# DeltaNet layer on one core: the solve's closing operations inside the scan's last step, and three matmul inputs at another offset

## The chip, the core and the metric

The kernel runs on one core of a Trainium2 chip. A core has five engines that each run their own list of instructions in order: PE (TensorE, matmuls into PSUM; PEld is its weight load), DVE (VectorE), ACT (ScalarE), POOL (GpSimd) and SP (SyncE, which issues the DMAs here). An instruction waits for semaphores that other engines or DMAs raise, and all that stands behind it on its engine waits with it. The metric is the device time of one execution in microseconds (us).

## What is computed

One transformer layer with a DeltaNet branch: 512 latent tokens, 256 context tokens, width 1024, everything in float32. The part that the change touches, cut from the reference:

```python
kk = jnp.einsum('bhncd,bhnsd->bhncs', k, k)
a_mat = jnp.where(strict, beta[..., :, None] * dec * kk, 0.0) + jnp.eye(GDN_CHUNK, dtype=jnp.float32)
uw = lax.linalg.triangular_solve(a_mat, rhs, left_side=True, lower=True, unit_diagonal=True)   # per chunk
def step(s, inp):                                                   # the scan over chunks
    delta = u_c - jnp.einsum('bhcd,bhde->bhce', w_c, s)
    s_new = gl_c[..., None, None] * s + jnp.einsum('bhcd,bhce->bhde', kd_c, delta)
    o = jnp.einsum('bhcd,bhde->bhce', qd_c, s) + jnp.einsum('bhcs,bhse->bhce', p_c, delta)
    return s_new, o
y = (jax.nn.sigmoid(g_a) * (attn @ w_pa) + jax.nn.sigmoid(g_d) * (gdn @ w_pd)) @ w_out         # output projection
x = x + g2 * ((jax.nn.silu(g) * val) @ w_down)                      # second MLP stage, after u = conv(h @ w_up)
```

The scan runs in both directions for 8 heads.

## The kernel before

Every large product is three matmuls: an fp32 value is split into a rounded part and a rest (hi and lo, tiles `whi`, `wlo` for weights; two halves for the moving input), and `mm3` sums hi·hi, hi·lo and lo·hi. The 128-column weight tiles come one after another by DMA (`wraw`); ACT makes `whi`, DVE makes `wlo`.

The program first makes modulations and normed inputs, then attention. After it comes the DeltaNet part, for the heads in four pairs p = 0 to 3, with 128-token chunks (6 for a pair and direction). A pair goes through two stages:

- `gdn_solve` and `gdn_solved` invert the 32x32 diagonal blocks of the triangular matrices. `gdn_solve` builds `C`, `X` and `R` (each 128x1024) and then runs 31 rounds of a product (`prod`) and a sum into `R`; these rounds are on POOL for the pairs 1 to 3. `gdn_solved` closes it with three operations on DVE: `R` times `gT`, and two block transposes of `R` into the tiles `o_tr` and `o_nt`. Then `gdn_inv` puts the blocks together to full inverses (tile `TTm`) with many small matmuls. It begins with 192 matmuls of 32x32 that read `o_tr`, `o_nt` and `NN` and write four PSUM banks.
- `gdn_scan` goes through six steps. In a step DVE makes `r`, PE makes `TTm` times `r` (bank `pds`), DVE copies that to `dl`, and PE makes `qT` times the state (bank `pq`), which DVE scales and adds into `oacc` (the first output sum, L117). In steps 4 and 5 PE multiplies the masks `M` with `dl` (bank `pe`) and DVE adds that into `oacc` (the second output sum, L108).

The PSUM tiles of both stages come from one ring of four banks (`pbank`, tag `pb`). The banks that `gdn_inv` takes first are those that the last scan step's `pq` and `pe` held, so that the first round of the 32x32 matmuls needs `o_tr`, `o_nt` and both output sums.

The solve of pair p+1 runs beside the inversion of pair p, and its rounds go on under the scan of pair p. What stands here as a *handover* is the place where the scan of pair p ends and the inversion of pair p+1 begins; there are three (p = 0 to 1, 1 to 2, 2 to 3). Between these pieces `weave` puts matmuls of the other projections on PE (`mb`, moving inputs `hxH`, `hxL`, then `at`), a fixed number per piece; it leaves none between the last `pe` matmuls and the first 32x32 matmuls. `put` pins the closing operations at their place in program order; much else on DVE, ACT, POOL and SP is placed by a scheduler.

After the pairs come the two branch projections (moving inputs `at` for attention, `g_*` for DeltaNet), the output projection (moving input `y`, matmuls into `mc`), the MLP's first stage (moving input `h`) and its second (moving input `a`). `two(pool, k, by, name)` makes the hi and lo halves of such an input: 2 x k rows of 2048 bytes in a partition, in one tile aligned to 2048 bytes, which begin `by` bytes behind the tile's start. `h` has 192, `y` 64 and `a` 256; `at` for heads 4 to 7 is a plain tile, thus 0.

Of the kernel before, what the change touches and what calls it, by code (L numbers as in the profile page):

```python
# [6 lines left out]
F32 = mybir.dt.float32  # L7
# [7 lines left out]
P = 128  # L15
D = 1024
KT = 8
# [61 lines left out]
def hybrid_layer_body(tc, x, ctxt, xT, consts, cols, rows, w_mod1, w_mod2, w_db, w_aq, w_cm, w_pa, w_pd, w_out,  # L79
# [54 lines left out]
    with es:  # L134
# [805 lines left out]
                        tt(R[:, j + 1:32, 0:n], R[:, j + 1:32, 0:n], pv, ALU.add, eng)  # L940
            pre.append(R)

        def gdn_solved(pre, keep):
            kT, gT, NN, R = pre
            put = tc.keep_in_program_order if keep else lambda i: i
            with solver():
                put(V.tensor_tensor(out=R, in0=R, in1=gT.unsqueeze(2).to_broadcast([P, 32, 32]), op=ALU.mult))
                outs = [gq.tile([P, 32, 32], F32, name=nm, align_bytes=2048, tag="q4", bufs=3) for nm in ("o_tr", "o_nt")]
                for o, r in zip(outs, (R, R.rearrange("p i k -> p k i"))):
                    put(V.transpose(o.rearrange("p u s -> p s u"), r))  # L950
            pre[3:] = outs

        def gdn_inv(p, pre):
            kT, gT, NN, o_tr, o_nt = pre
# [66 lines left out]
        def gdn_scan(p, pre, seqs, nxt):  # L1021
# [29 lines left out]
            for st in range(6):  # L1051
                lat = st >= 2
                if st == 2:
                    oacc = gpool[0].tile([P, 2, 4, P], F32, name="oacc", tag="oacc")
                pks, pds, rs_ = [None, None], [None, None], [None, None]
                for d in range(2):
                    c = seq[d][st]
                    if S[d] is not None:
                        pks[d] = pbank()
                        for hh in range(2):  # L1060
                            mm(pks[d][:, hh, :], kT[:, hh, c * P:(c + 1) * P], S[d][:, hh, :])
                if st > 0:
                    yield WS[0]
                for d in range(2):
                    c = seq[d][st]
                    if S[d] is not None:
                        r = gpool[0].tile([P, 2, P], F32, name="r", tag="r", bufs=2)
                        for hh in range(2):
                            u = hh * 6 + c
                            kc = cidx(d, hh, c)  # L1070
                            stt(r[:, hh, :], pks[d][:, hh, :], eg[:, kc:kc + 1], vtok[:, u, :], ALU.mult, ALU.subtract)
                        rs_[d] = r
                for d in range(2):
                    c = seq[d][st]
                    pds[d] = pbank()
                    for hh in range(2):
                        mm(pds[d][:, hh, :], TTm[:, d, hh * 6 + c, :], vtok[:, hh * 6 + c, :] if S[d] is None else rs_[d][:, hh, :])
                yield WS[1]
                for d in range(2):
                    c = seq[d][st]  # L1080
                    if st < 5:
                        dk = gpool[0].tile([P, 2, P], F32, name="dk", tag="dk", bufs=2)
                        for hh in range(2):
                            kc = cidx(d, hh, c)
                            act(dk[:, hh, :], pds[d][:, hh, :], AF.Copy,
                                scale=kdec[:, kc:kc + 1])
                    if lat:
                        dl = gpool[0].tile([P, 2, P], F32, name="dl", tag="dl", bufs=6)
                        V.tensor_copy(dl, pds[d][:, 0:2, :])
                        dls[(d, c)] = dl  # L1090
                    if st < 5:
                        pu = pbank()
                        for hh in range(2):
                            mm(pu[:, hh, :], ktok[:, hh * 6 + c, :], dk[:, hh, :])
                        Sn = gpool[0].tile([P, 2, P], F32, name="S", tag="S", bufs=4)
                        if S[d] is None:
                            ts(Sn, pu[:, 0:2, :], -1.0, ALU.mult)
                        else:
                            for hh in range(2):
                                kc = cidx(d, hh, c)  # L1100
                                stt(Sn[:, hh, :], S[d][:, hh, :], glast[:, kc:kc + 1], pu[:, hh, :], ALU.mult, ALU.add)
                    if lat:
                        pq = pbank()
                        for hh in range(2):
                            mm(pq[:, hh, :], qT[:, hh, (c - 2) * P:(c - 1) * P], S[d][:, hh, :])
                        for hh in range(2):
                            kc = cidx(d, hh, c)
                            if st < 4:
                                act(oacc[:, hh, c - 2, :], pq[:, hh, :], AF.Copy, scale=eg[:, kc:kc + 1])
                            else:  # L1110
                                stt(oacc[:, hh, c - 2, :], pq[:, hh, :], eg[:, kc:kc + 1], oacc[:, hh, c - 2, :], ALU.mult, ALU.add)
                    if st < 5:
                        S[d] = Sn
                if st == 5 and nxt is not None:
                    gdn_solved(nxt, True)
                yield WS[2]
                if st >= 1 and st < 5:
                    c = (4, 3, 5, 2)[st - 1]
                    PTs[c] = intra(c)
                if st >= 4:  # L1120
                    for d in range(2):
                        c = seq[d][st]
                        PT = PTs[c]
                        pe = pbank()
                        for hh in range(2):
                            mm(pe[:, hh, :], PT[:, 0, hh, :], dls[(0, c)][:, hh, :], True, False)
                            mm(pe[:, hh, :], PT[:, 1, hh, :], dls[(1, c)][:, hh, :], False, True)
                        tt(oacc[:, :, c - 2, :], oacc[:, :, c - 2, :], pe[:, 0:2, :], ALU.add)
# [71 lines left out]
        def filler():  # L1200
# [15 lines left out]
            atn = [None] * NH  # L1216

            def load_at(pool, h0):
                t = pool.tile([P, 8, NL], F32R, align_bytes=2048, name=f"at{h0}")
                H, L = t[:, 0:4], t[:, 4:8]  # L1220
                for i in range(4):
                    gt = atA.tile([P, NL], F32, name="gt", tag="gt", bufs=2)
                    SP.dma_start(gt, atd[h0 + i])
                    split(H[:, i, :], L[:, i, :], gt)
                    atn[h0 + i] = (H[:, i, :], L[:, i, :])
# [18 lines left out]
                finish_pa(c, pa)  # L1244
            pas_es.close()
            yp = y_es.enter_context(tc.tile_pool(name="yp", bufs=1, side="right", reuse_waits="tile"))
            yt.extend(two(yp, KT, 64, "y2"))

            def finish_pd(c, pd):
                yH, yL = yt  # L1250
# [94 lines left out]
        with ExitStack() as fe:  # L1345
# [70 lines left out]
            oe.close()  # L1416
            y_es.close()
            fp = fe.enter_context(tc.tile_pool(name="fp", bufs=1, side="right", reuse_waits="tile"))
            aH, aL = two(fp, NFF, 256, "a2")
            ups = [h * NFF + j for j in range(NFF) for h in range(2)]  # L1420
            banks = {}

# [171 lines left out]
```

## Time and profile before

| what | value |
|---|---|
| median of three runs | 1295.64 us (1291.88, 1295.64, 1295.73) |
| the profiled execution | 1298.42 us, of which 1296.3 us are the span from the first to the last instruction |
| PE busy | 1224.0 us (94% of the span) |
| DVE busy | 850.4 us (66%) |
| ACT busy | 625.5 us (48%) |
| POOL busy | 309.6 us (24%) |
| mean granted TensorE clock | 0.976 of full speed |
| chain that ended last, by engine | PE 70%, DVE 11%, DMA 6%, POOL 3%, issue 2%, ACT 2% |

The chain is followed back from the last instruction to whatever released each step, so its shares say on whom the end depended. Busy shares are averages over stages with different limits.

### The profile page before, as it was taken

The page shows a single profiled execution, that of the slowest core. Times are in us where ns is not written, and L with a number is a line of the kernel's source. Part 1 is how long each engine was busy: PE and PEld are TensorE (multiplying, and loading weights), DVE is VectorE, ACT ScalarE, POOL GpSimd, SP SyncE. Part 2 cuts the span into 40 slices and gives each one's busy share as a digit, 9 for nine tenths or more (in the row PEclk, how much of TensorE's full clock was granted, in tenths as well). Part 3 has the DMA queues.
Part 4 walks back from the last instruction along what each step waited for, and adds up shares of the span by engine and source line. Part 5 has one row for each costly group of instructions (what it writes and reads, how often), then busy time and mean ns, then how long its engine had stood idle before and what let it go on. Part 6 is the DMA issues. An engine that isn't in the chain of part 4 may idle for free.

```text
span 1296.3 us, 20844 instructions
## 1 busy us (share of the span) xinstructions
PE 1224.0 (94%) x7835; PEld 1031.7 (80%) x7835; DVE 850.4 (66%) x1625; ACT 625.5 (48%) x1403; POOL 309.6 (24%) x364
## 2 busy tenths in 40 slices
PE   7899999999988899799999799999999999999996
PEld 4487878899877778678888688888988888888886
DVE  5886987777779876685565556665676666663333
ACT  5453657665676665474353443233354444443221
POOL 1753430000123449649548300000000000000000
PEclk8999999999999999899899899999999999999999
DMA  8656631121253642543534555265043333233331
GB/s 326 220 170 203 217 127 62 66 86 45 100 189 126 189 159 86 171 126 115 171 107 138 163 165 172 97 223 176 15 130 98 98 98 98 97 94 89 92 99 66
DMA packets 70789, 170.81 MB, mean 132 GB/s; under 512 B 7872, under 2 KB 18720, under 8 KB 69280
## 3 DMA queue, kind: packets, MB, share of 16 engines
q1 hardware_dynamic: 70688, 169.47, 39.8%
q8 instruction: 62, 1.02, 0.3%
q14 instruction: 39, 0.32, 0.1%
HBM read 144.23 MB, written 25.21 MB: 131 GB/s over the span
## 4 chain that ended last, share of the span: by engine, by line
PE 70%; DVE 11%; DMA 6%; POOL 3%; issue 2%; ACT 2%; SPq 0%; POOLq 0%; DVEq 0%; ACTq 0%
PE mc L87 32%; PE mb L87 20%; PE pb L87 5%; PE pq L87 3%; PE pS L87 3%; PE ab L87 2%; DMA Gb<-gamdr 2%; DVE wlo L108 2%; PE ab L91 1%; PE pk L87 1%; DMA M<-gamdr 1%; PE xb L91 1%; DVE t L117 1%; POOL prod L108 1%; DMA wmd<-in_w_mod_dram 1%
## 5 line engine op out<-in xcount | busy, mean ns | idle before, releaser
L108 DVE TENSOR_TENSOR wlo<-wraw,whi 128x1024 fp32r<-128x1024 f32 x152 | 187.7, 1236 | 165.0 <-ACT whi L120 163.0
L120 ACT ACTIVATE whi<-wraw 128x1024 fp32r<-128x1024 f32 x152 | 158.8, 1048 | 207.9 <-PE mc L87 104.6
L87 PE MATMUL mc<-h,whi 128*128 128x512 f32 (+1 forms) x752 | 219.7, 376 | 0.3 <-ACT whi L120 0.3
L87 PE MATMUL mb<-hxH,whi 128*128 128x512 f32 x384 | 165.0, 430 | 2.6 <-DVE R L108 2.1
L87 PEld LDWEIGHTS mc<-h,whi 128*128 128x128 f32 x752 | 138.0, 188 | 25.9 <-ACT whi L120 0.5
L87 PE MATMUL mb<-hxH,wlo 128*128 128x512 f32 x384 | 154.1, 401 | 0.0
L87 PE MATMUL mb<-hxL,whi 128*128 128x512 f32 x384 | 153.8, 400 | 0.0
L87 PE MATMUL mc<-h,wlo 128*128 128x512 f32 (+1 forms) x376 | 141.3, 376 | 0.5 <-DVE wlo L108 0.5
L87 PE MATMUL mc<-a,whi 128*128 128x512 f32 (+1 forms) x396 | 111.4, 367 | 0.6 <-DVE x L117 0.6
L108 POOL TENSOR_TENSOR rc<-rc,mhalf 128x2 f32<-128x2 f32 x4 | 3.0, 741 | 454.4 <-DVE rc L114 454.4
L87 PEld LDWEIGHTS mb<-hxH,wlo 128*128 128x128 f32 x384 | 74.2, 193 | 17.2
L87 PEld LDWEIGHTS mb<-hxH,whi 128*128 128x128 f32 x384 | 75.1, 196 | 13.7 <-ACT t L120 2.3
L87 PEld LDWEIGHTS mb<-hxL,whi 128*128 128x128 f32 x384 | 75.1, 196 | 10.1
L87 PEld LDWEIGHTS mc<-a,whi 128*128 128x128 f32 x396 | 71.4, 188 | 13.1 <-DVE x L117 0.8
L87 PEld LDWEIGHTS mc<-h,wlo 128*128 128x128 f32 x376 | 70.8, 188 | 13.8 <-DVE wlo L108 1.0
L87 PE MATMUL mc<-a,wlo 128*128 128x512 f32 (+1 forms) x198 | 72.7, 367 | 0.0
L117 DVE SCALAR_TENSOR_TENSOR u<-mc,col,u 128x511 f32<-128x511 f32 x88 | 65.4, 747 | 1.4
L108 POOL TENSOR_TENSOR prod<-X,R 128x31 f32<-128x31 f32 (+15 forms) x93 | 57.5, 618 | 23.6 <-DVE X L108 16.7
L87 PE MATMUL pq<-whi,hxH 128*128 128x256 f32 x192 | 56.1, 292 | 0.0
L108 POOL TENSOR_TENSOR R<-R,prod 128x31 f32<-128x31 f32 (+15 forms) x93 | 53.6, 577 | 6.8
L87 PE MATMUL pq<-wlo,hxH 128*128 128x256 f32 x192 | 54.3, 283 | 0.4 <-DVE wlo L108 0.4
L87 PE MATMUL pq<-whi,hxL 128*128 128x256 f32 x192 | 54.1, 282 | 0.0
(346 smaller groups left out, 2870.5 us busy)
## 6 DMA issues: line engine op xcount, KB each, us to landing
wraw<-in_w_cm_dram SPq DMA_DIRECT2D x48, 512.0 KB, 4.0
wraw<-in_w_up_dram SPq DMA_DIRECT2D x44, 512.0 KB, 3.7
wmd<-in_w_mod_dram SPq DMA_DIRECT2D x64, 256.0 KB, 3.8
wm<-in_w_mod_dram SPq DMA_DIRECT2D x8, 1024.0 KB, 8.0
wraw<-in_w_down_dram SPq DMA_DIRECT2D x16, 512.0 KB, 3.5
wraw<-in_w_aq_dram SPq DMA_DIRECT2D x12, 512.0 KB, 4.8
M<-gamdr SPq DMA_DIRECT2D x64, 64.0 KB, 4.2
wraw<-in_w_pa_dram SPq DMA_DIRECT2D x8, 512.0 KB, 4.1
```

The source lines that it names most:

```text
L87: i = nc.tensor.matmul(*a, **k)
L91: i = nc.tensor.transpose(*a, **k)
L108: (eng or V).tensor_tensor(out=out, in0=a, in1=b, op=op)
L117: V.scalar_tensor_tensor(out=out, in0=a, scalar=s, in1=b, op0=op0, op1=op1)
L120: A.activation(out, a, f, **kw)
```

## The change

`gdn_solved` is cut in two: part 0 is the product `R` times `gT`, part 1 the two transposes (before, all three stood behind the last scan step's first output sums). In the last step (st 5) part 0 now stands behind `r`, ahead of the matmuls with `TTm`, and part 1 behind the second `dl` copy, ahead of the output sums. Three offsets change: `at` of heads 4 to 7 from 0 to 192 bytes (its tile becomes 512 bytes longer per partition), `y` from 64 to 192, `a` from 256 to 192.

```diff
-        def gdn_solved(pre, keep):
-            kT, gT, NN, R = pre
+        def gdn_solved(pre, keep, part=None):
             put = tc.keep_in_program_order if keep else lambda i: i
             with solver():
-                put(V.tensor_tensor(out=R, in0=R, in1=gT.unsqueeze(2).to_broadcast([P, 32, 32]), op=ALU.mult))
-                outs = [gq.tile([P, 32, 32], F32, name=nm, align_bytes=2048, tag="q4", bufs=3) for nm in ("o_tr", "o_nt")]
-                for o, r in zip(outs, (R, R.rearrange("p i k -> p k i"))):
-                    put(V.transpose(o.rearrange("p u s -> p s u"), r))
-            pre[3:] = outs
+                if part != 1:
+                    kT, gT, NN, R = pre
+                    put(V.tensor_tensor(out=R, in0=R, in1=gT.unsqueeze(2).to_broadcast([P, 32, 32]), op=ALU.mult))
+                if part != 0:
+                    R = pre.pop()
+                    pre += [gq.tile([P, 32, 32], F32, name=nm, align_bytes=2048, tag="q4", bufs=3) for nm in ("o_tr", "o_nt")]
+                    for o, r in zip(pre[3:], (R, R.rearrange("p i k -> p k i"))):
+                        put(V.transpose(o.rearrange("p u s -> p s u"), r))
...
                         rs_[d] = r
+                if st == 5 and nxt is not None:
+                    gdn_solved(nxt, True, 0)
                 for d in range(2):
                     c = seq[d][st]
                     pds[d] = pbank()
...
                         V.tensor_copy(dl, pds[d][:, 0:2, :])
                         dls[(d, c)] = dl
+                    if st == 5 and d and nxt is not None:
+                        gdn_solved(nxt, True, 1)
                     if st < 5:
...
-                if st == 5 and nxt is not None:
-                    gdn_solved(nxt, True)
                 yield WS[2]
...
             def load_at(pool, h0):
-                t = pool.tile([P, 8, NL], F32R, align_bytes=2048, name=f"at{h0}")
-                H, L = t[:, 0:4], t[:, 4:8]
+                if h0:
+                    H, L = two(pool, 4, 192, "at4")
+                else:
+                    t = pool.tile([P, 8, NL], F32R, align_bytes=2048, name="at0")
+                    H, L = t[:, 0:4], t[:, 4:8]
...
-            yt.extend(two(yp, KT, 64, "y2"))
+            yt.extend(two(yp, KT, 192, "y2"))
...
-            aH, aL = two(fp, NFF, 256, "a2")
+            aH, aL = two(fp, NFF, 192, "a2")
```

The order of PE's instructions is the same in both kernels. On DVE the three handovers change. First handover (pair 0 to 1), before: what DVE runs behind the last step's `dl` copies (`t`, `co` and `wlo` belong to the woven projections; a number behind x counts equal neighbours).

```order
L108 TENSOR_TENSOR wlo<-wraw,whi 128x1024
L117 SCALAR_TENSOR_TENSOR oacc<-pb,eg,oacc 128x128 x2
L117 SCALAR_TENSOR_TENSOR t_6057<-mb,col,t_6057 128x511
L117 SCALAR_TENSOR_TENSOR oacc<-pb,eg,oacc 128x128 x2
L947 TENSOR_TENSOR R<-R,gT 128x1024
L117 SCALAR_TENSOR_TENSOR t_6057<-mb,col,t_6057 128x511
L108 TENSOR_TENSOR oacc<-oacc,pb 128x2x128
L950 STREAM_TRANSPOSE o_tr<-R 128x32x32
L950 STREAM_TRANSPOSE o_nt<-R 128x32x32
L892 STREAM_TRANSPOSE gT<-g 128x32
L108 TENSOR_TENSOR oacc<-oacc,pb 128x2x128
```

The same place of DVE in the changed kernel, from the end of `r`:

```order
L949 TENSOR_TENSOR R<-R,gT 128x1024
L892 STREAM_TRANSPOSE gT<-g 128x32
L1094 COPY dl<-pb 128x256 x2
L954 STREAM_TRANSPOSE o_tr<-R 128x32x32
L954 STREAM_TRANSPOSE o_nt<-R 128x32x32
L114 TENSOR_SCALAR rkq_186<-gkss 128x4
L108 TENSOR_TENSOR wlo<-wraw,whi 128x1024
L117 SCALAR_TENSOR_TENSOR oacc<-pb,eg,oacc 128x128 x2
L117 SCALAR_TENSOR_TENSOR t_6057<-mb,col,t_6057 128x511
L117 SCALAR_TENSOR_TENSOR oacc<-pb,eg,oacc 128x128 x2
L117 SCALAR_TENSOR_TENSOR t_6057<-mb,col,t_6057 128x511
L108 TENSOR_TENSOR oacc<-oacc,pb 128x2x128 x2
```

The product moved ahead of the `dl` copies, the transposes ahead of all output sums, and the two second output sums now follow each other with no transposes between or ahead of them. Second handover (pair 1 to 2) on DVE, before, from `r`:

```order
L117 SCALAR_TENSOR_TENSOR r<-pb,eg,vtok 128x128 x4
L108 TENSOR_TENSOR wlo<-wraw,whi 128x1024
L1089 COPY dl<-pb 128x256 x2
L117 SCALAR_TENSOR_TENSOR oacc<-pb,eg,oacc 128x128 x4
L947 TENSOR_TENSOR R<-R,gT 128x1024
L950 STREAM_TRANSPOSE o_tr<-R 128x32x32
L950 STREAM_TRANSPOSE o_nt<-R 128x32x32
L108 TENSOR_TENSOR oacc<-oacc,pb 128x2x128 x2
```

And in the changed kernel:

```order
L117 SCALAR_TENSOR_TENSOR r<-pb,eg,vtok 128x128 x4
L949 TENSOR_TENSOR R<-R,gT 128x1024
L108 TENSOR_TENSOR wlo<-wraw,whi 128x1024
L1094 COPY dl<-pb 128x256 x2
L954 STREAM_TRANSPOSE o_tr<-R 128x32x32
L954 STREAM_TRANSPOSE o_nt<-R 128x32x32
L117 SCALAR_TENSOR_TENSOR oacc<-pb,eg,oacc 128x128 x4
L108 TENSOR_TENSOR oacc<-oacc,pb 128x2x128 x2
```

The product moved up by three rows, the transposes ahead of the four first output sums. Third handover (pair 2 to 3) on DVE, before:

```order
L1089 COPY dl<-pb 128x256 x2
L117 SCALAR_TENSOR_TENSOR oacc<-pb,eg,oacc 128x128 x3
L108 TENSOR_TENSOR wlo<-wraw,whi 128x1024
L117 SCALAR_TENSOR_TENSOR oacc<-pb,eg,oacc 128x128
L947 TENSOR_TENSOR R<-R,gT 128x1024
L108 TENSOR_TENSOR oacc<-oacc,pb 128x2x128
L950 STREAM_TRANSPOSE o_tr<-R 128x32x32
L950 STREAM_TRANSPOSE o_nt<-R 128x32x32
L108 TENSOR_TENSOR oacc<-oacc,pb 128x2x128
```

And in the changed kernel:

```order
L949 TENSOR_TENSOR R<-R,gT 128x1024
L1094 COPY dl<-pb 128x256 x2
L954 STREAM_TRANSPOSE o_tr<-R 128x32x32
L954 STREAM_TRANSPOSE o_nt<-R 128x32x32
L117 SCALAR_TENSOR_TENSOR oacc<-pb,eg,oacc 128x128 x3
L108 TENSOR_TENSOR wlo<-wraw,whi 128x1024
L117 SCALAR_TENSOR_TENSOR oacc<-pb,eg,oacc 128x128
L108 TENSOR_TENSOR oacc<-oacc,pb 128x2x128 x2
```

All three operations moved ahead of the first output sum. Behind the handovers the scheduler also moves some `M` masks, small `rkq` factors and `TTm` copies on ACT and POOL by a few rows.

## Rows read from the trace of the kernel before

**Rows 1.** Busy time by stretch (PE, PEld, DVE, ACT, POOL in us with counts, then granted TensorE clock, DMA share, GB/s): a stretch inside a scan, and the one with the first handover.
```profile
600.00:625.00 25.00, 25.00 (x160) 22.35 (x159) 13.61 (x36) 10.24 (x26) 21.72 (x36) 1.00 0.29 96
525.00:550.00 25.00, 17.08 (x177) 14.82 (x177) 14.20 (x27) 13.59 (x47) 13.40 (x24) 0.80 0.54 175
```

**Rows 2.** Timeline of the first handover (start us, duration us, engine, line, operation, out<-in, count, then idle time of the engine before it and who ended it).
```profile
524.80 1.13 DVE L117 SCALAR_TENSOR_TENSOR r<-pb,eg,vtok 128x128 f32<-128x128 f32 x4
...
526.15 0.25 POOL L108 TENSOR_TENSOR R<-R,prod 128x31 f32<-128x31 f32 x1
...
528.20 0.87 DVE L1089 COPY dl<-pb 128x256 f32<-128x256 f32 x2 [2.28 <-PE pb L87]
...
533.32 1.05 ACT L120 ACTIVATE whi<-wraw 128x1024 fp32r<-128x1024 f32 x1
...
533.49 1.95 PE L87 MATMUL pb<-dl,M 128*128 128x128 f32 x16
...
534.86 1.22 DVE L108 TENSOR_TENSOR wlo<-wraw,whi 128x1024 fp32r<-128x1024 f32 x1
...
536.00 0.60 DVE L117 SCALAR_TENSOR_TENSOR oacc<-pb,eg,oacc 128x128 f32<-128x128 f32 x2
...
536.52 0.74 DVE L117 SCALAR_TENSOR_TENSOR t<-mb,col,t 128x511 f32<-128x511 f32 x1
...
537.70 1.22 DVE L947 TENSOR_TENSOR R<-R,gT 128x1024 f32<-128x1024 f32 x1
...
539.49 0.41 DVE L108 TENSOR_TENSOR oacc<-oacc,pb 128x256 f32<-128x256 f32 x1
...
541.59 2.00 DVE L950 STREAM_TRANSPOSE o_nt<-R 128x1024 f32<-128x1024 f32 x1
...
543.98 0.26 PE L87 MATMUL pb<-o_nt,NN 32*32 32x32 f32 x1
```

**Rows 3.** Timeline of the second handover: the last rounds of the solve on POOL end first.
```profile
624.21 0.25 POOL L108 TENSOR_TENSOR R<-R,prod 128x31 f32<-128x31 f32 x1
...
629.60 1.13 DVE L117 SCALAR_TENSOR_TENSOR r<-pb,eg,vtok 128x128 f32<-128x128 f32 x4
...
637.17 1.95 PE L87 MATMUL pb<-dl,M 128*128 128x128 f32 x16
...
641.41 0.74 DVE L108 TENSOR_TENSOR oacc<-oacc,pb 128x256 f32<-128x256 f32 x2
...
642.21 0.26 PE L87 MATMUL pb<-o_nt,NN 32*32 32x32 f32 x1
```

**Rows 4.** Timeline of the third handover.
```profile
712.06 0.25 POOL L108 TENSOR_TENSOR R<-R,prod 128x31 f32<-128x31 f32 x1
...
722.03 1.12 DVE L117 SCALAR_TENSOR_TENSOR r<-pb,eg,vtok 128x128 f32<-128x128 f32 x4
...
728.71 1.95 PE L87 MATMUL pb<-dl,M 128*128 128x128 f32 x16
...
729.60 1.04 ACT L120 ACTIVATE whi<-wraw 128x1024 fp32r<-128x1024 f32 x1
...
737.84 0.25 PE L87 MATMUL pb<-o_nt,NN 32*32 32x32 f32 x1
```

**Rows 5.** Busy time by stretch (columns as in rows 1): PE's work behind each handover at the lower clock level, from the end of the 32x32 matmuls on, and two stretches of the scan of pair 1.
```profile
545.40:549.20 3.80, 3.80 (x15) 3.41 (x14) 2.07 (x5) 3.32 (x17) 3.51 (x7) 0.50 0.19 69
643.60:648.20 4.60, 4.60 (x19) 3.99 (x16) 1.46 (x3) 4.51 (x21) 4.18 (x9) 0.50 0.30 57
739.20:743.80 4.60, 4.60 (x17) 3.57 (x12) 1.79 (x4) 4.01 (x20) 4.36 (x8) 0.50 0.01 2
...
576.00:586.00 10.00, 9.01 (x53) 7.71 (x54) 4.85 (x9) 6.18 (x22) 7.48 (x13) 1.00 0.60 199
586.00:594.00 8.00, 5.41 (x21) 4.22 (x20) 5.41 (x8) 3.52 (x9) 7.47 (x9) 0.79 0.31 99
```

**Rows 6.** Matmuls into `mc` alone by stretch (PE busy us with the count, granted clock, DMA share, GB/s): the output projection (`y`), the MLP's first stage (`h`) and second stage (`a`), 512 columns each, then the output projection's half-width matmuls (256 columns).
```profile
873.00:900.00 27.00, 27.00 (x118) 1.00 0.56 187
950.00:1150.00 200.00, 200.00 (x884) 1.00 0.31 97
1165.00:1260.00 95.00, 95.00 (x417) 1.00 0.33 96
901.00:911.00 10.00, 10.00 (x88) 1.00 0.45 152
```

**Rows 7.** Timeline of PE: half-width matmuls of the MLP's first stage (the first and the last of a run of 21, up to the second row's start), and 512-column matmuls with `at` (the two rows' starts are three matmuls apart).
```profile
918.98 0.40 PE L87 MATMUL mc<-h,whi 128*128 128x256 f32 x2
...
921.50 0.40 PE L87 MATMUL mc<-h,whi 128*128 128x256 f32 x2
...
801.30 0.39 PE L87 MATMUL mb<-at,wlo 128*128 128x512 f32 x1
...
801.99 0.39 PE L87 MATMUL mb<-at,wlo 128*128 128x512 f32 x1
```

**Rows 8.** Timeline in the scan of pair 1: a DMA for a later pair's masks, what waits behind it on DVE, and PE's wait for `r`.
```profile
576.27 0.38 SPq L899 DMA_DIRECT2D Gb<-gamdr  x1
...
586.88 1.99 DVE L117 SCALAR_TENSOR_TENSOR co<-co,t 128x512 f32<-128x512 f32 x1 [3.37 <-ACT co L120]
...
589.18 1.41 PE L87 MATMUL pb<-r,TTm 128*128 128x128 f32 x8 [2.59 <-DVE r L117]
```

## The prediction, made before the changed kernel ran

> **What bounds the kernel now.** I read the page first: PE is busy for 94% of the span and has 70% of the chain that ended last, DVE 11%. So time is won where PE stands still or runs slowly, and nowhere else. The busy time by stretch shows where: inside a scan PE works 25.00 of 25 us, in the stretch with the first handover 17.08, at a granted clock of 0.80 [rows 1]. The timelines of the three handovers then show for whom PE stands still [rows 2 to 4]. After the last matmuls with `dl`, PE has nothing woven in; its next work, the 32x32 matmuls, needs `o_tr`, `o_nt` and all four output sums, since it takes the banks these sums read. All of that stands on DVE in one line. In the first handover the solve's rounds on POOL end at 526.40, but DVE begins the product only at 537.70, behind a `wlo` that waits for ACT's `whi` (ends 534.37) and behind output sums; PE's last `dl` matmul ends at 535.44 and its stream runs from 543.98, when the last output sum frees the last bank [rows 2]. In the second handover PE ends at 639.12 and streams from 642.21 [rows 3], in the third from 730.66 and 737.84 [rows 4]. That is 8.5, 3.1 and 7.2 us without real work. Behind each handover PE then runs for 3.8, 4.6 and 4.6 us at half clock [rows 5].
>
> **The change part by part.** It adds and removes no work on PE, DVE, ACT or in the DMA queue that I price; it moves three DVE operations and three inputs. PE's order does not change, so each term is a wait that gets shorter or a pace that changes.
>
> First handover. I lay the new DVE order over the old trace, with its durations [rows 2]. `r` ends at 525.93, POOL's last round at 526.40: the product (1.22) ends at 527.6. This is the wait the change adds: `dl` stands behind it. But `dl` waits for PE until 528.20 anyway, so the 0.5 us for POOL costs nothing. `dl` ends at 529.1, two transposes of at most 2.00 end at 533.1. `wlo` still waits for `whi` until 534.37 and ends at 535.6. Then two output sums (0.60), `t` (0.74), two sums (0.60), `t` (0.74) and the two second sums (0.41 each): 3.5 us, to 539.1. PE's stream begins there instead of at 543.98: **4.9 us**. The transposes are hidden under PE's woven matmuls and ACT's work; what PE waits for next is the output sums, late because of `whi`.
>
> Second handover [rows 3]. `r` ends at 630.73, the solve was done at 624.46. Product to 631.95, `wlo` (1.22 as in rows 2) to 633.2, `dl` (at most 0.87) to 634.0, transposes to 638.0, four first sums (twice 0.60) to 639.2. PE's last `dl` matmul ends at 639.12, so the second sums (0.74 in all) run to about 639.9 at the latest and 639.6 at the earliest; 639.7 instead of 642.21: **2.5 us**.
>
> Third handover [rows 4]. `r` ends at 723.15, the solve at 712.31. Product to 724.4, `dl` to 725.3, transposes to 729.3, three sums to 730.2. `wlo` waits for `whi` until 730.64 and ends at 731.9; one sum (0.3) and the two second sums bring it to 733.0 instead of 737.84: **4.8 us**.
>
> Together 12.2 us. A gain only lasts if what comes behind comes earlier too. Behind the handovers PE is the bound again, and the loads of the next pair start when PE's inversion frees their tiles, so I let the whole pass. Bounds: nothing of it, or all.
>
> Clock. At the lower level work takes twice as long, so the three half-clock stretches cost 1.9, 2.3 and 2.3 us [rows 5]. After the change the standstills are about 3.7, 0.6 and 2.3 us. The scan of pair 1 has one of each kind: around a short wait the clock stays at 1.00, and in the stretch where PE waits 2.59 us for `r` it is 0.79 [rows 5, 8]. So I take the second handover's loss as gone and the others as staying: **2.3 us**, with bounds 0 and 6.5.
>
> Moved inputs. A 512-column matmul lasts 0.39 us and the next starts 0.23 after it, so a window counts some 1.7 that began before it. Thus one start in (27 / 116.3) = 232.2 ns with `y` (offset 64), 200 / 882.3 = 226.7 with `h` (192), 95 / 415.3 = 228.7 with `a` (256) [rows 6], and 0.69 / 3 = 230 with `at` [rows 7]. If the offset sets the pace and 192 gives 226.7 everywhere, the 120 wide matmuls with `y` (5 tiles x 24) win 0.66 us, the 462 with `a` (7 x 66) 0.92, the 96 with the moved `at` 0.3. Against that, half-width matmuls: 10 us hold some 85.6 with `y`, 117 ns each [rows 6]; `h` takes 2.52 / 21 = 120 [rows 7]; with the 276 of `y` and `a` that gives back 0.8. Net **1.1 us**; bounds: 0.8 lost (only the half-width effect) and 1.9 won.
>
> A rule speaks against this term. The rows show three paces for one shape at one granted clock of 1.00 [rows 6]. The Trainium skill, "SBUF — State Buffer", section "Who interferes with whom", says that PE never waits for another engine's access, and "TensorE: Matmul & The Clock Gate", section "Back-to-back issue gap", makes the spacing of isolated matmuls a matter of the column count (about 216 ns for 512). By these the offset would do nothing and the term would be 0; the trace disagrees in that the paces differ, but no run here shows yet that the offset is the cause: `y` also ran under a DMA share of 0.56, `h` and `a` under 0.31 and 0.33.
>
> Sum: 12.2 + 2.3 + 1.1 = 15.6 us, from the profiled execution's 1298.42 to 1282.8. That execution stood 2.8 us over the median of the runs, so against the median 1295.64 I predict **1280.0**.
>
> **Rivals.** (a) *The moves do nothing*, because the pace follows DMA traffic or the weights: `a` and `h` with a like DMA share but 2.0 ns apart speak against it, `y`'s traffic for it. Without the term of 1.1: 1281.1. [...]
>
> (b) *The gain is handed back at the next load.* In the scan of pair 1 a mask load issued at 576.27 ends in a wait of ACT and DVE, and PE waits 2.59 us for `r` [rows 8]. If such loads don't come earlier with PE, the first two handovers' 7.4 us become a longer wait there. For it: the SP queue runs in order, and the load stands behind others. Against it: what it waits for is freed by PE and DVE, which are earlier. 1287.4.
>
> (c) *The clock comes back altogether*: all three standstills stay short enough. Then 6.5 instead of 2.3: 1275.8. The 2.59 us wait speaks against it.
>
> (d) *POOL becomes the bound, and the kernel slower.* The product now holds DVE ahead of `dl` until POOL has finished. In the first handover POOL ends 0.47 us after `r`; DVE has 1.3 us to spare until `whi` comes (533.1 to 534.37). From there each us of a later POOL costs one; from 6.2 us on, the handover is slower than before. POOL would have to come some 25 us later than now for 1303.6 (25 - 1.3 = 23.7 over 1280). In the other two it ends 6.3 and 10.8 us ahead of `r`, and POOL works on the same inputs as before, so I see no cause for it.
>
> (e) *The change does not bite*: DVE's line ends no earlier since the output sums end it anyway. That is true of the last half us only: 539.1, 639.7 and 733.0 already count them. With that half us and the moved inputs alone, 1.1 + 0.5, about 1294.
>
> **Chances and range.** The forecast 0.54, (a) 0.18, (b) 0.18, (c) 0.05, (d) 0.02, (e) 0.03. Forecast and (a) alone lie within 1278 to 1283. The range goes from below (c), with the inputs' best bound, to (b): 1274 to 1288. A difference of 0.3%, 3.9 us, is about what a measurement of this kernel can tell from none. All cases but (d) and (e) are faster by more: faster 0.94 (I take 0.01 off for mixtures), same 0.04, slower 0.02.
>
> **What the changed profile would show.** The product starting behind `r` in each handover and not held by POOL for more than 1 us; the 32x32 matmuls starting within 4, 1 and 3 us of the last `dl` matmul, ended by an output sum and not by a transpose; full clock behind the second handover; the pace with `y` and `a` at 226 to 227 ns. It would be wrong if PE's wait for `r` in the scan of pair 1 grew by about the first handover's gain (b), if DVE idled ahead of the product (d), or if `y` and `a` kept their paces (a).

## The result, and the profile after

The changed kernel took 1276.85 us (median of 4 runs, 1270.96 to 1279.78). Beside it the kernel before took 1295.1 (4 runs), so the ratio is 0.9859 with a 95% interval of 0.9838 to 0.988: 18.2 us less, 15.5 to 21.0. The forecast was 1280.0 in a range of 1274 to 1288. The profiled execution of the changed kernel has a span of 1275.0 us at a mean granted clock of 0.983, against 1296.3 at 0.976.

Busy time by stretch in the changed kernel (columns as in rows 1): the stretch of the first handover, one inside a scan, what follows on the three handovers, and the stretch in the scan of pair 1 behind PE's wait for `r`.

```profile
525.00:550.00 25.00, 23.24 (x303) 19.66 (x303) 18.87 (x34) 15.59 (x51) 14.91 (x23) 0.93 0.59 183
600.00:625.00 25.00, 25.00 (x159) 22.35 (x159) 15.75 (x40) 7.98 (x19) 16.21 (x28) 1.00 0.35 107
539.60:543.00 3.40, 3.40 (x12) 2.83 (x11) 1.70 (x5) 2.52 (x12) 2.26 (x4) 0.50 0.51 162
629.50:634.50 5.00, 4.67 (x121) 4.10 (x120) 2.92 (x8) 3.96 (x20) 3.57 (x7) 1.00 0.97 318
720.50:724.00 3.50, 3.50 (x10) 2.67 (x10) 1.06 (x3) 2.75 (x13) 1.33 (x3) 0.51 0.58 154
585.00:595.00 10.00, 10.00 (x64) 8.85 (x64) 5.65 (x16) 4.05 (x14) 9.14 (x14) 1.00 0.40 141
```

The first row answers to the second of [rows 1]: PE works 23.24 of 25 us instead of 17.08, at 0.93 instead of 0.80. The scan's inside is as it was. The third to the sixth row answer to [rows 5]: half clock is left for 3.4 us behind the first and the third handover, none behind the second, and none in the scan of pair 1.

Timelines of the changed kernel's first handover (to be laid beside [rows 2]), first DVE, then PE.

```profile
526.38 1.23 DVE L949 TENSOR_TENSOR R<-R,gT 128x1024 f32<-128x1024 f32 x1 [0.23 <-POOL R L108]
...
528.45 0.87 DVE L1094 COPY dl<-pb 128x256 f32<-128x256 f32 x2 [0.59 <-PE pb L87]
529.24 2.05 DVE L954 STREAM_TRANSPOSE o_tr<-R 128x1024 f32<-128x1024 f32 x1
531.14 2.12 DVE L954 STREAM_TRANSPOSE o_nt<-R 128x1024 f32<-128x1024 f32 x1
...
533.86 1.22 DVE L108 TENSOR_TENSOR wlo<-wraw,whi 128x1024 fp32r<-128x1024 f32 x1 [0.60 <-ACT whi L120]
...
537.35 0.74 DVE L108 TENSOR_TENSOR oacc<-oacc,pb 128x256 f32<-128x256 f32 x2
...
533.74 1.95 PE L87 MATMUL pb<-dl,M 128*128 128x128 f32 x16
535.66 0.24 PE L87 MATMUL pb<-o_tr,NN 32*32 32x32 f32 x2
536.83 0.24 PE L87 MATMUL pb<-o_nt,NN 32*32 32x32 f32 x2 [0.93 <-DVE oacc L117]
537.82 0.24 PE L87 MATMUL pb<-o_tr,NN 32*32 32x32 f32 x2 [0.74 <-DVE oacc L108]
538.15 0.21 PE L87 MATMUL pb<-o_nt,NN 32*32 32x32 f32 x1
```

The product stands behind `r` and waits for POOL for 0.23 us; the transposes end at 533.26, before `whi` does. PE has its `dl` matmuls done at 535.69 and streams from 538.15, so 2.46 us without real work, where it was 8.5. Both waits inside are ended by `oacc`, none by a transpose.

The other two handovers on PE in the changed kernel (beside [rows 3, 4]).

```profile
628.49 1.94 PE L87 MATMUL pb<-dl,M 128*128 128x128 f32 x16
...
630.95 0.21 PE L87 MATMUL pb<-o_nt,NN 32*32 32x32 f32 x1 [0.33 <-DVE oacc L108]
...
714.80 1.95 PE L87 MATMUL pb<-dl,M 128*128 128x128 f32 x16
...
718.19 0.24 PE L87 MATMUL pb<-o_nt,NN 32*32 32x32 f32 x2 [1.27 <-DVE oacc L117]
...
718.85 0.21 PE L87 MATMUL pb<-o_nt,NN 32*32 32x32 f32 x1
```

From the end of the `dl` matmuls to the stream: 0.5 us instead of 3.1, and 2.1 instead of 7.2. Laying the two traces over each other matmul by matmul, the changed kernel runs ahead by 7.1 us over the first handover and the half clock behind it, 2.1 in the scan of pair 1, 5.2 over the second, 6.1 over the third, and 1.4 in the stages with `y` and `a`: about 22, of which the two executions' own distance to their medians takes some 3.

### The profile page after: what moved, and what is told of

It is laid out like the page before. It is cut to its first block, busy times and chain, and to the rows that moved or that the text cites. A ratio compares the mean times of both kernels' runs of the same rounds, so it can differ in the third digit from the quotient of the medians.

```text
span 1275.0 us, 20851 instructions
## 1 busy us (share of the span) xinstructions
PE 1217.5 (95%) x7835; PEld 1027.1 (81%) x7835; DVE 849.0 (67%) x1625; ACT 624.2 (49%) x1403; POOL 308.5 (24%) x364
## 4 chain that ended last, share of the span: by engine, by line
PE 70%; DVE 12%; DMA 5%; ACT 3%; POOL 3%; issue 2%; SPq 0%; POOLq 0%; DVEq 0%; ACTq 0%
PE mc L87 32%; PE mb L87 20%; PE pb L87 5%; PE pq L87 3%; PE pS L87 3%; PE ab L87 3%; DVE wlo L108 2%; DMA Gb<-gamdr 2%; PE ab L91 1%; DMA M<-gamdr 1%; DVE macc L377 1%; PE pk L87 1%; PE xb L91 1%; DVE qt L108 1%; POOL prod L108 1%
```

## The experiments

**The handovers alone.** The changed kernel without the moved inputs:

```diff
-                if h0:
-                    H, L = two(pool, 4, 192, "at4")
...
-            yt.extend(two(yp, KT, 192, "y2"))
+            yt.extend(two(yp, KT, 64, "y2"))
...
-            aH, aL = two(fp, NFF, 192, "a2")
+            aH, aL = two(fp, NFF, 256, "a2")
```

> The changed kernel with the three inputs back at their old offsets: only the closing operations of the solve are moved. If the handovers carry the change, the three standstills and the stretches at half clock are as in the changed kernel (PE's 32x32 stream from about 538, the second handover at full clock), and the time is 16 to 18 us under the kernel before: 1277 to 1279, 1.5 us over the changed kernel, the share that the paces with y and a have in its trace (0.6 + 1.0 us). If the moved inputs carry more than their paces show, for instance by shifting a stage, it is 1282 or more.

Measured: 1276.26 us (4 runs), ratio 0.9859 (0.9841 to 0.9878). The handovers carry all that the times can tell; the 1.5 us that were expected over the changed kernel are less than the intervals resolve. In this execution the third handover is at full clock, the first is not (stretches behind the third and the first, columns as in rows 1):

```profile
720.00:724.00 4.00, 4.00 (x68) 3.08 (x69) 0.98 (x4) 3.92 (x15) 0.71 (x3) 1.00 0.48 141
540.70:544.00 3.30, 3.30 (x11) 2.74 (x11) 1.70 (x5) 2.46 (x11) 2.54 (x4) 0.50 0.56 163
```

The order is the changed kernel's, but not quite the standstill: at the third handover PE streams 1.8 us after its `dl` matmuls here (716.53 to 718.31) and 2.1 us after them in the changed kernel, since `whi` came 0.3 us earlier against PE.

**The inputs alone.** The kernel before with the three new offsets (the diff above, the other way, on the old order).

> The kernel before with only the three inputs at their new offsets; its instructions stand in the old order on every engine. If the offset sets the pace (the forecast's term of 1.1 us): one 512-column matmul starts every 226.7 ns with y and with a, instead of 232.2 and 228.7, and the time is 1 to 1.7 us under before, 1293.5 to 1294.5, too little for the times to tell, so the paces decide. If rival (a) holds and DMA traffic or the weights set the pace, y stays at 232 and a at 228.7. at4: the forecast's 230 to 226.7 ns, or 230 as in the changed kernel's trace.

Measured: 1291.84 us (12 runs), ratio 0.998 (0.9968 to 0.9993), 0.9 to 4.1 us less. Matmuls into `mc` in this kernel: the stretches with `y` and `a` (busy PE with the count, granted clock, DMA share, GB/s):

```profile
863.50:890.50 27.00, 26.98 (x119) 1.00 0.57 194
...
1155.00:1250.00 95.00, 95.00 (x420) 1.00 0.33 97
```

The first window begins with the stage's first matmul, so 27 / 119 = 226.9 ns with `y`; 95 / (420 - 1.7) = 227.1 with `a`. All the rest of the stage is as before, its DMA share too (0.57, and 0.56 before): the offset is the cause, and rival (a) falls. With `at4` nothing was won: its neighbouring matmuls start 230.1 ns apart on average before and 231.3 in the changed kernel (72 distances each, those with narrow matmuls of the inversion between them left out), and single distances go from 224 to 237 ns at either offset. Why the offset doesn't show there stays open.

**All at the worst offset.** The changed kernel with `y2`, `a2` and `h2` at 64:

```diff
-            h2H, h2L = two(h2p, KT, 192, "h2")
+            h2H, h2L = two(h2p, KT, 64, "h2")
```

> The changed kernel with the inputs y, h and a all at offset 64 (at4 stays at 192). If the offset sets the pace, h and a take the 232.2 ns that y had there before: 984 + 462 + 120 wide matmuls x 5.5 ns = 8.6 us, less up to some 1 us for the half-width ones: 7 to 9 us slower than the changed kernel, about 1285. If the pace follows DMA traffic, weights or the tile, h and a stay at 226.7, y goes back to 232 or not, and the time is within 1 us of the changed kernel.

Measured: 1287.35 us (6 runs), ratio 0.9935 (0.9915 to 0.9955), 9.8 us over the changed kernel's ratio; laid over its trace, the stages with `y`, `h` and `a` lose 8.4. `h` and `a` here:

```profile
930.00:1130.00 200.00, 200.00 (x862) 1.00 0.30 95
1149.00:1244.00 95.00, 95.00 (x411) 1.00 0.32 94
```

200 / (862 - 1.7) = 232.5 ns and 95 / (411 - 1.7) = 232.1: `h`, with a DMA share of 0.30 as before, takes on the pace that `y` had at 64.

**Other offsets.** The changed kernel with `y2` at 448, `h2` at 320 and `a2` at 128.

> The changed kernel with y at 448, h at 320 and a at 128 instead of 192. Paces seen so far for 512 columns: 232 ns at 64, 226.7 at 192, 228.7 at 256. If 192 is singular, all three are slower than 226.7; if what counts is only that 64 is bad, all three stand at 227 to 229. The time follows from the paces: each ns is 1.6 us over y, h and a.

Measured: 1283.63 us (4 runs), ratio 0.9926 (0.9896 to 0.9956). `y`, `h` and `a`:

```profile
852.30:879.30 27.00, 26.87 (x119) 1.00 0.55 195
930.00:1130.00 200.00, 200.00 (x863) 1.00 0.29 95
1150.00:1245.00 95.00, 95.00 (x409) 1.00 0.32 96
```

226.9 ns at 448, 232.2 at 320, 233.2 at 128. Neither theory of the expectation is right: 448 is as good as 192, 320 as bad as 64. In both pairs that were tried, offsets 256 bytes apart have the same pace.

**The product at the transposes' place.** All three operations behind the `dl` copies:

```diff
-                if st == 5 and nxt is not None:
-                    gdn_solved(nxt, True, 0)
...
-                        gdn_solved(nxt, True, 1)
+                        gdn_solved(nxt, True)
```

> The changed kernel with the product no longer at once behind r: product and transposes all stand behind the dl copies and ahead of the output sums. PE still needs 1 to 3 us of matmuls with S and dl before the handover. If the transposes ahead of the output sums are what counts and the product's own place is worth little, the first handover is covered (DVE idled for whi and for dl there), the other two lose up to the product's 1.2 us each where DVE had waited for dl anyway: 0 to 2.5 us over the changed kernel, 1277 to 1279.5. If the early product carries the gain, the 1.2 us per handover come back in full, with half clock behind the second handover again (2.3 to 2.6): 5 to 7 us over it, 1282 to 1284.

Measured: 1284.44 us (4 runs), ratio 0.9909 (0.9886 to 0.9931), 6.5 us over the changed kernel's. That is the second theory's number, but not by its mechanism. DVE in the first handover of this kernel:

```profile
531.49 1.21 DVE L949 TENSOR_TENSOR R<-R,gT 128x1024 f32<-128x1024 f32 x1
535.61 0.17 DVE L114 TENSOR_SCALAR rkq<-gkss 128x4 f32<-128x4 f32 x1 [2.91 <-ACT xb L120]
535.69 2.00 DVE L954 STREAM_TRANSPOSE o_tr<-R 128x1024 f32<-128x1024 f32 x1
```

The scheduler puts a 0.17 us `rkq` between product and transposes, which waits 2.91 us for ACT; behind it the transposes and the output sums stand where PE already waits. Of the 7.6 us that this trace loses against the changed kernel's from the first handover on, 4.3 are lost here, 2.0 in the scan of pair 1 and 1.3 in the other two handovers. In this trace the early product's worth in the first handover is that nothing slow slips in front of the transposes.

**The transposes at their old place.** Only the product early:

```diff
-                    if st == 5 and d and nxt is not None:
-                        gdn_solved(nxt, True, 1)
...
+                if st == 5 and nxt is not None:
+                    gdn_solved(nxt, True, 1)
                 yield WS[2]
                 if st >= 1 and st < 5:
```

> The changed kernel with the two transposes back behind the first output sums; the product stays behind r in the last step. If the transposes' place carries the handovers: in the first, the sums and the second t end at 536.8 in the changed kernel's trace and 3.9 us of transposes come behind them, so PE's stream starts about 4 us later; in the second about 1, in the third 3 to 4; with the clock that comes to 8 to 12 us over the changed kernel, 1285 to 1289. If the early product carries them (with product and transposes both behind dl the time was 7.6 us over the changed kernel), this stays within 2 us of it, 1277 to 1279.

Measured: 1286.17 us (10 runs), ratio 0.9955 (0.9934 to 0.9975), 12.4 us over the changed kernel's. PE in its first handover waits for both transposes again:

```profile
531.79 1.95 PE L87 MATMUL pb<-dl,M 128*128 128x128 f32 x16
537.59 0.31 PE L87 MATMUL pb<-o_tr,NN 32*32 32x32 f32 x2 [3.85 <-DVE o_tr L954]
539.39 0.31 PE L87 MATMUL pb<-o_nt,NN 32*32 32x32 f32 x2 [1.49 <-DVE o_nt L954]
```

The transposes ahead of the output sums carry two thirds of the change (12.4 of 18.2 us). The first theory holds. The other 5.8 us would be the moved inputs' (1.4 in the traces) and the early product's if the parts added up; they don't quite, since the early product's place alone cost 6.5.

**The product one step earlier.** `if st == 5` to `if st == 4` at the product.

> The changed kernel with the product one step of the scan earlier; on DVE it then stands ahead of the last two sums and r of the first handover, while POOL's rounds end at 526.35 in the changed kernel's trace. If rival (d) is a real mechanism, only not met by the change: DVE idles about 2.4 us ahead of the product in the first handover, r comes 3 us later and PE waits for it, and the later line gains the product's 1.2 us back; in the other two handovers nothing changes, since POOL is done long before. 2 to 5 us over the changed kernel, 1279 to 1282. If a held DVE costs nothing here because PE has woven matmuls in front: 1276 to 1278.

Measured: 1274.53 us (4 runs), ratio 0.9879 (0.9856 to 0.9901): no difference that these runs can tell from the changed kernel. DVE, then PE, in the first handover:

```profile
525.40 1.23 DVE L949 TENSOR_TENSOR R<-R,gT 128x1024 f32<-128x1024 f32 x1 [2.55 <-POOL R L108]
...
527.33 1.08 DVE L117 SCALAR_TENSOR_TENSOR r<-pb,eg,vtok 128x128 f32<-128x128 f32 x4
...
527.70 1.26 PE L87 MATMUL pb<-r,TTm 128*128 128x128 f32 x8 [0.70 <-DVE r L117]
```

Rival (d)'s mechanism is there: POOL holds DVE for 2.55 us and `r` with it. But PE waits only 0.70 for `r`, since woven matmuls stand in front. Laid over the changed kernel's trace, 1.1 us are lost there and 0.7 come back at the handover, and behind it the clock stays full in this execution. The prediction's rule that from 1.3 us on each us of a later POOL costs one is not tested by this: POOL ended when it did, and only DVE reached the product earlier.

**Weaving more work into the standstill.** `W1` from 0 to 3 in the changed kernel, and from 0 to 10 in the kernel before.

> The changed kernel with three pieces of woven projection (9 matmuls of 512 columns, 2.07 us) between the scan and the inversion. If PE's standstill at the handover is still a cost (2.2, 0.6 and 1.9 us left in the changed kernel's trace), the pieces fill it and are missing nowhere else: 3 to 5 us faster, and up to 2 more where half clock goes: 1271 to 1274. If the pieces are missing later, where they had covered a wait, or hold back the inversion and with it the next load: 1276 to 1280.

> The kernel before, with the solve's closing operations in the old place, and ten pieces of woven projection (30 matmuls, 6.9 us) between scan and inversion. If the cost of the old order was PE's standstill and nothing else, woven work fills it as well as the new order shortens it: of 8.5, 3.1 and 7.2 us some 6.9, 3.1 and 6.9 are filled, and with the clock the time is 1275 to 1280. If the pieces are missing later in the scans, part of it comes back: 1283 to 1290. If the late inversion itself was the cost (the next pair's loads and solve hang on it), the time stays near before, 1292 or more.

Measured: 1281.4 us (4 runs), ratio 0.9929 (0.991 to 0.9948), 9 us worse than the changed kernel (the two profiled executions differ by 4); and 1294.38 (10 runs), ratio 1.0028 (1.0012 to 1.0044), slower than before. In the changed kernel with weaving, the handover's stretch (first row) is at full clock with PE busy for 36.17 of 37 us, as hoped. The second row is the end of the last pair's scan, where the changed kernel has PE busy for 39.24 of 40 us at 1.00:

```profile
523.00:560.00 37.00, 36.17 (x440) 30.38 (x440) 30.84 (x64) 23.18 (x69) 16.70 (x29) 1.00 0.57 187
790.00:830.00 40.00, 33.65 (x175) 27.25 (x175) 20.27 (x51) 8.04 (x23) 1.64 (x1) 0.91 0.26 86
```

The woven projections are a fixed stock; what is spent at the handovers is missing at the end, where PE stands still for longer and at a lower clock. In the kernel before it is the same (stretch 815 to 845: PE busy for 21.29 of 30 us at a clock of 0.72, and 29.24 at 1.00 without the weaving).

**The clock by itself.** The kernel before, with transposes of the identity that nobody reads, between scan and inversion:

```diff
-            weave(wait(W1), 1.0)
+            if p + 1 < NP:
+                for _ in range((14, 5, 14)[p]):
+                    xb = xbank()
+                    for i in range(4):
+                        transpose(xb[:, i, :], ident)
```

> The kernel before with 56, 20 and 56 transposes of the identity, which nobody reads (about 6.1, 2.2 and 6.1 us at 109 ns each), put between scan and inversion in the three handovers: PE is busy there, but does nothing of use and the line on DVE is as long as before. If the half clock behind the handovers comes from PE's standing still and is a cost of its own: PE's 32x32 stream starts when it did, the clock stays at 1.00 behind all three handovers, and the time is 4 to 8 us under before (half of 10.2 + 6.8 + 10.2 us of half clock is 13.6 at most; the forecast's term had it at 6.5). If the half clock comes from something else, or the extra transposes only hold up the stream: the same as before or slower.

Measured: 1289.26 us (12 runs), ratio 0.9988 (0.9975 to 1.0001). PE's filling in the first and the third handover, and DVE's last output sum of the third:

```profile
533.70 9.87 PE L91 MATMUL xb<-cst 128*128 128x128 f32 x56
...
721.99 9.87 PE L91 MATMUL xb<-cst 128*128 128x128 f32 x56
731.79 0.21 PE L87 MATMUL pb<-o_tr,NN 32*32 32x32 f32 x1
...
727.16 0.40 DVE L108 TENSOR_TENSOR oacc<-oacc,pb 128x256 f32<-128x256 f32 x1
```

And the stretches behind the three handovers (columns as in rows 1):

```profile
544.00:547.00 3.00, 3.00 (x77) 2.70 (x64) 0.83 (x2) 3.00 (x18) 2.73 (x6) 1.00 0.25 93
638.00:642.00 4.00, 4.00 (x21) 3.33 (x20) 1.18 (x2) 3.94 (x20) 3.67 (x8) 1.00 0.45 86
732.50:736.50 4.00, 4.00 (x52) 3.31 (x41) 1.11 (x2) 1.20 (x3) 1.92 (x2) 1.00 0.02 4
```

All three stand at full clock, where [rows 5] have 0.50, although the line on DVE is the old one; and over the 12 executions the mean granted clock was 0.986 to 0.993, beside 0.977 to 0.990 in the 19 of the kernel before. That the half clock follows from PE's standstill is thereby shown. The gain, 1.7 us (3.2 less to 0.1 more), is smaller than expected because the filling was too long: in the third handover PE filled on for 4.2 us after the last output sum. Laid over the trace of before, 1.2 and 2.5 us are won over the first and the second handover and 0.1 over the third; another 3.3 are won in the scan of pair 1, where nothing was filled. A transpose took 9.87 / 56 = 176 ns on average and not 109. Within a group of four they do start 109 ns apart; but the first weight load of each group waits for the semaphore that the last transpose of the group before raises, and 0.3 us go by before it.

**The same for the changed kernel**, sized by that number: `(3, 0, 2, 0)[p]` groups of four.

> The changed kernel with 12 transposes of the identity, which nobody reads, ahead of the inversion in the first handover and 8 in the third (175 ns each as in the kernel before with such filling: 2.1 and 1.4 us, as long as PE stands there in the changed kernel's trace, 2.2 and 1.9). If the half clock that is left behind these two handovers (3.4 us each) comes from that standing still: full clock there, 1.7 us less each, 1 to 3.5 us faster than the changed kernel, 1273 to 1276. If what is left of half clock comes and goes with other things: within 1 us of it, or slower by what the filling holds up.

Measured: 1269.13 us (5 runs, 1267.88 to 1269.78), ratio 0.9818 (0.9796 to 0.984): 5.3 us under the changed kernel's ratio, the fastest of all. PE in its first handover, and the stretch of 25 us around it:

```profile
532.61 2.03 PE L91 MATMUL xb<-cst 128*128 128x128 f32 x12
534.57 0.24 PE L87 MATMUL pb<-o_tr,NN 32*32 32x32 f32 x2
...
535.76 0.24 PE L87 MATMUL pb<-o_tr,NN 32*32 32x32 f32 x2 [0.74 <-DVE oacc L108]
...
525.00:550.00 25.00, 24.06 (x335) 19.96 (x333) 19.84 (x41) 19.20 (x61) 14.62 (x20) 1.00 0.54 184
```

There is no half clock anywhere from the first handover to the end of the scans. Laid over the changed kernel's trace, 5.7 us are won from there to the end of the scans: 1.4 over the first handover, 0.8 in the scan of pair 1, 2.1 over the third handover, 1.4 where PE had waited for `dk` in the last scan. The two waits in the scans (for `r`: 1.25 us instead of 2.07 of idle time) were not touched by the edit; that they are shorter can be their own scatter. The gain is above the 1 to 3.5 us expected: the half clock of the changed kernel's profiled execution could give back 3.4 at most. The two intervals just touch, so how much of 5.3 is the clock and how much scatter stays open.

**Output sums ahead of the weight split.** The last step's sums in the changed kernel under `with sooner()`.

> The changed kernel with the last step's output sums ranked ahead of weight splits on DVE; only in the third handover does that move an instruction (the fourth first sum now stands ahead of a wlo that waits for ACT). If output sums queued behind wlo are the next thing PE waits for: PE's stream in the third handover starts up to 1.2 us earlier, and the rest is as in the changed kernel: 1 to 2 us faster at most, 1275 to 1277. If the dl matmuls end last anyway: the same start and time.

Measured: 1273.56 us (5 runs), ratio 0.9862 (0.984 to 0.9883): no change. DVE in the third handover:

```profile
717.56 1.11 DVE L117 SCALAR_TENSOR_TENSOR oacc<-pb,eg,oacc 128x128 f32<-128x128 f32 x4
718.55 1.48 DVE L108 TENSOR_TENSOR wlo<-wraw,whi 128x1024 fp32r<-128x1024 f32 x1
719.96 0.74 DVE L108 TENSOR_TENSOR oacc<-oacc,pb 128x256 f32<-128x256 f32 x2
```

The split now stands between the first and the second sums, and PE waits for the second ones instead. The theory that sums behind `wlo` are what is late next was not refuted; the edit only moved the split by one place. PE does stream 0.7 us earlier behind its `dl` matmuls here, but `whi` was 0.8 us earlier too. ACT makes `whi` only behind masks for which POOL waits on a DMA (`M` from `gamdr`: 0.64 us in the changed kernel, 0.83 here), so the line that is late next goes back to that load.

## Why the prediction was right, point by point

**The bound.** Right: PE's standstill in the three handovers, ended by DVE's line, was what could be won. With the transposes alone put back 12.4 us return; with the inputs alone put back nothing measurable does.

**The three handovers, 12.2 us.** The standstills shrank by 6.1, 2.6 and 5.1 us, 13.8 together; the terms were 4.9, 2.5 and 4.8. The miss of the first, 1.2 us, comes mostly from holding `whi` at its old end: ACT's `whi` ended at 533.82 and not at 534.37 (533.57 in the old trace's time), since the mask that ACT works on ahead of it came 0.8 us earlier by the same measure, and the rest of the line was 0.4 us shorter because neighbouring rows overlap a little and their durations were added up. What PE waits for next, output sums behind `wlo`, is as said.

**The gain passes on.** Right. The load of [rows 8] came 6.8 us earlier with the rest. PE's wait for `r` there was 2.07 us instead of 2.59, but it goes from 0.69 to 2.67 over the runs without more weaving, whatever the order, so this difference says nothing; rival (b), which saw the wait grow by 7.4 us, is out in every one of them.

**Clock, 2.3 us.** The mechanism was right and is now shown (the filling), the size was read from one execution. The pair of profiles differs by about 6: half clock fell from 10.2, 6.8 and 10.2 us to 3.4, 0 and 3.4, and 1.6 us of it were in the scan of pair 1, where the prediction let it stay. But the scatter is large. The granted clock in the traces gives these half-clock stretches (us). They count PE's standing still too: of before's 10.2, 6.8 and 10.2 us PE was busy 5.8, 6.5 and 6.5.

| kernel | 1st handover | scan of pair 1 | 2nd | 3rd |
|---|---|---|---|---|
| before | 10.2 | 3.4 | 6.8 | 10.2 |
| inputs alone (old order) | 6.8 | 3.4 | 0 | 6.8 |
| transposes back | 6.8 | 3.4 | 0 | 6.8 |
| product at the transposes' place | 6.8 | 3.4 | 0 | 3.4 |
| before, filled | 0 | 0 | 0 | 0 |
| changed | 3.4 | 0 | 0 | 3.4 |
| handovers alone | 3.4 | 0 | 0 | 0 |
| changed, all at 64 | 3.4 | 0 | 0 | 3.4 |
| changed, other offsets | 3.4 | 0 | 0 | 0 |
| changed, output sums first | 3.4 | 3.4 | 0 | 0 |
| changed, product at step 4 | 0 | 0 | 0 | 0 |
| changed, filled | 0 | 0 | 0 | 0 |

At the second handover of the old order PE streams 3.1 us after its `dl` matmuls in two executions, with 6.8 us of half clock in before [rows 3, 5] and none in the kernel with the inputs alone (PE in the latter, then the stretch behind the handover):

```profile
631.69 1.95 PE L87 MATMUL pb<-dl,M 128*128 128x128 f32 x16
...
636.72 0.21 PE L87 MATMUL pb<-o_nt,NN 32*32 32x32 f32 x1
...
638.00:642.00 4.00, 4.00 (x22) 3.40 (x22) 0.83 (x2) 3.92 (x20) 3.58 (x9) 1.00 0.27 71
```

The medians leave 18.2 - 13.8 - 1.4 = 3.0 us for the clock and all else, near the term; as 18.2 is only known to within 2.8 us, this does not confirm its size. What the step got wrong is to treat each handover's half clock as kept or lost; it comes in part, and not in every execution.

**Moved inputs, 1.1 us.** The wide matmuls with `y` and `a` won 0.7 and 1.0 us, as said. `at4` won nothing of its 0.3, and the half-width matmuls gave back 0.1 with `y` (88 in 10 us, before and after) and 0.2 to 0.3 with `a` where 0.8 was set for both; so 1.4 stands against 1.1. That it comes so near is luck: these two misses go opposite ways. Rival (a) is refuted by the inputs alone and by `h` at 64. The Trainium skill, "TensorE: Matmul & The Clock Gate", section "Back-to-back issue gap", gives the spacing of isolated matmuls by the column count alone. That does not carry over to the streams here, where the runs show 226.9 to 233.2 ns for one shape by the moving input's offset alone. The Trainium skill's "SBUF — State Buffer", section "Who interferes with whom", by which PE never waits for another engine's access, is not contradicted: at offset 64 the pace was 232.2 ns under a DMA share of 0.56 and 232.5 under 0.30.

**Rivals (c), (d), (e).** (c), the clock back altogether, did not come with the change in its profiled execution, but comes with 20 transposes that nobody reads, and with them the time is 5.3 us lower (the intervals just touch). (d): POOL held the product for 0.23 us; 2.55 us, at a product one step earlier, cost nothing that the times show, and a later POOL was not tried. (e): the output sums do end the line, but 6.1, 2.6 and 5.1 us earlier.

**The median.** The correction of 2.8 us for the profiled execution of before was needed: the pair of profiles differs by 21.6 us, the medians by 18.2.

## What to carry to other kernels

At a handover between two stages, look for short operations whose inputs have long been ready and which an in-order engine only reaches behind operations that wait; put them where that engine waits anyway, and check in the new order what the scheduler slips between them. Filling a standstill with useful work from a fixed stock moves the standstill to where the stock ends. Where a standstill remains and the rows behind it show half clock, filling it with throwaway matmuls, no longer than the wait itself, gave the clock back in this kernel; size them by their duration in that very place, the waits between their groups included.

## What the runs showed of the hardware

In the output projection and both MLP stages (`y`, `h`, `a`) the pace of 512-column fp32r matmuls depends on the byte offset at which the moving input begins, in tiles aligned to 2048 bytes: 232 ns at 64 and 320, 233 at 128, 226.7 to 227 at 192 and 448, 228.7 at 256. The two pairs 256 bytes apart agree. Over the 1,566 such matmuls with `y`, `h` and `a`, 64 instead of 192 cost 8.4 us in the traces and 9.8 by the ratios. For `at4` the move to 192 changed nothing (230.1 and 231.3 ns), and what makes the pace depend on the offset no run shows.

128-column transposes of the identity start 109 ns apart within a group of four that writes one tile. In a row of 14 such groups through the same pool PE's first weight load of a group waited for the end of the group before, which makes 176 ns each on average.
